# A backward scan in place of a reciprocal, and the early token sums moved into the low-rank products, in a hybrid HGRN2 and latent-attention layer

## The chip, the cores and the metric

The kernel runs on one core of a Trainium2 chip. The metric is the device time of one execution in microseconds (us). The engines are called PE (matrix products; PEld is its weight load), DVE (vector), ACT (scalar, with the function tables), POOL (GpSimd) and SP (which here only issues DMAs). A granted clock of 1.00 is PE at full speed.

## The reference

One decoder layer on 512 tokens of width 1024, all in 32-bit floats. The input is normalized and multiplied by one wide matrix, whose columns feed two branches and a merge:

```
h = rms_norm(x);  P = h @ w_in
f = lb + (1 - lb) * sigmoid(hf);  k = 1 - f;  q = silu(hq);  v = hi      # HGRN2, 8 heads of 128
b = cumsum(log f) inside each chunk of 32 tokens
q_in = q * exp(b);  k_in = k * exp(-b);  k_out = k * exp(b_last - b)
o = causal(q_in @ k_in^T) @ v + q_in @ state                            # state: over the chunks
y_a = rms_norm(o) * silu(z_a)
y_b = attention(c_q, c_kv, k_rope) * silu(z_b)                          # 8 heads, low-rank q and kv
m = sigmoid(g_a) * (y_a @ w_proj_a) + sigmoid(g_b) * (y_b @ w_proj_b)
out = x + m @ w_out
```

Along a token chunk, exp(b) is the running product of f, and exp(b_last - b) is the product of the f that come after a token up to the chunk's end.

## The kernel before, in words

Every product is made in three terms. A 32-bit matrix is split into a high part (a cast on ACT, L129 and L171) and a low part (what is left, on DVE, L130 and L172), and `mm3` issues high by high, high by low and low by high (L102 to L104). Normalized tokens lie transposed in `hT[0]` and `hT[1]`, the high and the low part, features on the partitions. Weights come by `load_w`: SP issues a load of 512 KB into one of three raw buffers (L123), ACT casts, DVE subtracts. Behind each load SP pops one DMA of a list `queued` (L790): a copy of a part of the merge's weights into DRAM scratch (`g_t`), to which POOL adds another part later, one `step()` at a time (L797). These sums of weights, and sums of token blocks, serve the merge products at the end, which are made by a scheme of the Strassen kind.

The order of the work: the norm with the first low-rank columns (c_q and a part of c_kv), written out by hand; then the "wide low-rank products", 448 columns more in four token tiles (`mm_ps` to `c_sb`, L400 is ACT's copy of a tile); the squares and norms of these (L405 on ACT, `power` on POOL, L418 on DVE); their transposes on PE (L422), cast and split into `cT` (L423 and L424); the rotated key part `kd` (L411 to L415 on POOL), its transposes (L428) and its split into `kpe`. Then come the HGRN heads, in four pairs, and after them the attention heads and the merge. Apart from the hand-ordered stretches, the scheduler of the kernel's framework sets the order on each engine, from the priorities of the program's order and a model of costs.

A pair of heads (`hg_pair`) makes the product of its forget columns F (two PSUM tiles of `mm_ps`, of which there are three in all), then `hg_forget` for both heads, then the values I (for four heads at a time), the query columns Q, `hg_query`, the state products, the gate columns ZA, the scores and the outputs. `hg_forget` goes so: tanh on ACT (L460) out of PSUM, `f` on DVE (L461), `k` on POOL (L463), the running product `pr` by a scan on DVE (L465), whose second operand `fr` restarts it at each chunk, its reciprocal over all 512 columns (L466), ten small POOL operations on the chunk ends (`gh`, `ft`), then `ki = k / pr` (L483), `ko = ki * last` (L484), `k64` and `k128`. The tile of tanh and the reciprocal share one buffer (`tf`), `f` and the query share another, so that the second head's tanh waits for the first head's `ki`. The scores use `ki` against `qi` within blocks of 64 tokens (L532), `ko` against `qi` from chunk to chunk, and `k64` against `q64`.

The tiles of the heads lie in a pool `hgrn`, among them `fr`, two `gh` and two `asb` (the score tiles, cleared once by POOL, L439 to L445). The pool's space is free early in the kernel, so these clearings run at 16 to 17.5 us.

`early_sums(q)` makes, for one half of the feature tiles, the sums of the token blocks of `hT` that the merge needs: four sums of high and low part (L820), four combinations (L773 and L777), a split of each into high and low, and eight stores of 256 KB from SP (L827). Its tiles are those of the attention's pool `mla_a`. The call for the first half stands in the first pair, where the other pairs call `step()`; that for the second half stands behind the first pair.

Of the kernel before, what the change touches and what calls it, by code (L numbers as in the profile page):

```python
# [24 lines left out]
C = 32  # L25
# [5 lines left out]
TINY = 1.1754944e-38  # L31
# [7 lines left out]
def hybrid_layer(ctx: ExitStack, tc: tile.TileContext, a):  # L39
    nc = tc.nc  # L40
# [11 lines left out]
    dram = ctx.enter_context(tc.tile_pool(name="dram", bufs=1, space=bass.MemoryType.DRAM))  # L52
# [114 lines left out]
    last_pool, last_dve, last_act = [None], [None], [None]  # L167

    def split(hi, lo, src):

        nc.scalar.copy(hi, src)  # L171
        nc.vector.tensor_tensor(lo, src, hi.bitcast(F32), op=ALU.subtract)  # L172
# [283 lines left out]
    def hg_forget(h, pf, meanwhile=None):  # L456

        gh = gh_[h % 2]
        tf, f, k = W("tf", 1), W("f", 1), W("k", 1)
        nc.scalar.activation(tf[:], pf[:], AF.Tanh, scale=0.5)  # L460
        nc.vector.tensor_scalar(f[:], tf[:], c1[:, h : h + 1], c2[:, h : h + 1], op0=ALU.mult, op1=ALU.add)  # L461
        nc.gpsimd.tensor_scalar(fr[:, ::C], f[:, ::C], TINY, None, op0=ALU.max)
        nc.gpsimd.tensor_scalar(k[:], tf[:], c1n[:, h : h + 1], c1[:, h : h + 1], op0=ALU.mult, op1=ALU.add)  # L463
        pr, rp = W("pr"), W("tf", 1)
        nc.vector.tensor_tensor_scan(pr[:], f[:], fr[:], 0.0, op0=ALU.mult, op1=ALU.max)  # L465
        nc.vector.reciprocal(rp[:], pr[:])  # L466
# [12 lines left out]
        last_pool[0] = g.tensor_tensor(ft[:], gh[:, :, 6], gh[:, :, 1], op=ALU.mult)
        if meanwhile:  # L480
            meanwhile()
        ki, ko, k128, k64 = W("ki"), W("ko"), W("k128"), W("k64", 2, (P, S // 2))
        nc.vector.tensor_tensor(ki[:], k[:], rp[:], op=ALU.mult)  # L483
        nc.vector.tensor_tensor(c3(ko), c3(ki), last.rearrange("p (n o) -> p n o", o=1).broadcast_to([P, S // C, C]), op=ALU.mult)  # L484
        last_pool[0] = g.tensor_tensor(c2_(k64), c4(ko)[:, :, 0:2], bc(gh, 8, 2), op=ALU.mult)
        nc.vector.tensor_tensor(c4(k128), c4(ko), bc(gh, 0, 4), op=ALU.mult)
        return pr, ft, ki, ko, k64, k128

    def hg_query(h, pq, pr, meanwhile=None):

        gh = gh_[h % 2]
        q = W("f", 1)
        last_act[0] = nc.scalar.activation(q[:], pq[:], AF.Tanh, scale=0.5)
        if meanwhile:
            meanwhile()
        nc.vector.scalar_tensor_tensor(q[:], q[:], 1.0, pq[:], op0=ALU.add, op1=ALU.mult)
# [4 lines left out]
        return qi, q64, q128  # L501

    n3 = (NT - 1) * P

# [20 lines left out]
    def hg_scores(heads):  # L525

        res = [(asb_[h % 2], ax_tile()) + t for h, t in heads]
        for _, aps, ki, ko, k64, qi, q64 in res:
# [5 lines left out]
        for _, aps, ki, ko, k64, qi, q64 in res:  # L534
# [5 lines left out]
        for asb, aps, ki, ko, k64, qi, q64 in res:  # L540
# [231 lines left out]
    def minus(out, x, y):
        nc.vector.tensor_tensor(out, x, y, op=ALU.subtract)  # L773

    def minus_minus(out, x, y):

        nc.vector.scalar_tensor_tensor(out, x, -1.0, y, op0=ALU.mult, op1=ALU.subtract)  # L777
# [33 lines left out]
    h_dram = [[dram.tile([P, 4, 256], F32, name=f"h{n}{i}") for i in range(2)] for n in range(1, 5)]  # L811

    def early_sums(q):

        E = lambda tag: ma_pool.tile([P, 2, 256], F32, tag)[:]
        h11, h12, h21, h22 = zip(*[[b[:, q] for b in blocks(t)] for t in hT])

        def whole(tag, hl):
            out = E(tag)
            nc.vector.tensor_tensor(out, hl[0].bitcast(F32), hl[1].bitcast(F32), op=ALU.add)  # L820
            return out

        def keep(n, tag, src):
            hl = Pair(ma_pool.tile([P, 2, 2, 256], F32R, tag)[:])
            split(*hl, src)
            for i in range(2):
                nc.sync.dma_start(h_dram[n - 1][i][:, q], hl[i].bitcast(F32))  # L827

        e22, e21, e11, e12 = whole("qr", h22), whole("qs", h21), whole("qh", h11), whole("p3", h12)
        minus(e22, e22, e21)  # L830
        keep(1, "qn", e22)
        minus_minus(e22, e22, e11)
        keep(2, "kn", e22)
        minus(e21, e11, e21)
        keep(3, "qp", e21)
        minus_minus(e12, e12, e22)
        keep(4, "qn", e12)
# [470 lines left out]
```

## Time and profile before

| | |
|---|---|
| median of 3 executions | 606.26 us (606.16 to 606.81) |
| the profiled execution | 606.53 us, of which the span is 604.7 us |
| mean granted clock of PE | 0.996 |
| PE busy | 595.2 us (98%) |
| DVE busy | 445.2 us (74%) |
| ACT busy | 283.0 us (47%) |
| POOL busy | 148.3 us (25%) |

The profile is a page with busy shares, and a trace that answers queries: waits (an engine's idle time by what ended it), stretches (busy time of each engine between two times), groups of instructions by line, and timelines. In a timeline row the first number is the start and the second the length in us, and in brackets stands the idle time of the engine before it, with what ended it. A matmul of 512 columns reads 0.39 us long, but the next one starts 0.23 us after it, since they overlap. Every time below is from the start of the span.

### The profile page before, as it was taken

How to read it: one execution, taken by the hardware profiler on the slowest of the kernel's cores; microseconds unless marked ns; L12 is line 12 of the kernel's file. 1: busy time of each engine (PE TensorE's matmuls, PEld its weight loads, DVE VectorE, ACT ScalarE, POOL GpSimd, SP SyncE). 2: the span in 40 equal slices, each digit the busy share in tenths (PEclk: the TensorE clock that was granted, in tenths of full speed). 3: DMA queues.
4: the chain of work that ended last, by engine and by line, in shares of the span. 5: the costliest groups of instructions: out<-in, count | busy, mean ns of one | idle time of the engine just before them, and what ended most of it. 6: DMA issues, size and time to landing. Idle time of an engine off the chain costs nothing.

```text
span 604.7 us, 8828 instructions
## 1 busy us (share of the span) xinstructions
PE 595.2 (98%) x3198; PEld 501.5 (83%) x3198; DVE 445.2 (74%) x689; ACT 283.0 (47%) x517; POOL 148.3 (25%) x253
## 2 busy tenths in 40 slices
PE   9999999999999999999999999999999999999994
PEld 6998888888888888888888888888888888888883
DVE  7717989599764548959767776778878878466795
ACT  7555245333313342436545554456557764153553
POOL 3107322254350237415245540400000000000003
PEclk9999999999999999999999999999999999999998
DMA  8449479997969967582369676888666656366313
GB/s 281 159 137 345 155 220 370 318 223 169 239 152 253 232 194 155 112 186 76 62 153 175 147 159 154 222 289 244 192 187 204 204 182 188 123 233 257 102 36 139
DMA packets 73036, 115.34 MB, mean 191 GB/s; under 512 B 7561, under 2 KB 37663, under 8 KB 72993
## 3 DMA queue, kind: packets, MB, share of 16 engines
q1 hardware_dynamic: 63740, 90.99, 47.2%
q0 software_dynamic: 8336, 22.55, 20.2%
q10 hardware_dynamic: 916, 1.25, 0.6%
q8 instruction: 25, 0.41, 0.3%
q14 instruction: 19, 0.15, 0.1%
HBM read 106.38 MB, written 39.85 MB: 242 GB/s over the span
## 4 chain that ended last, share of the span: by engine, by line
PE 89%; DVE 4%; DMA 3%; ACT 2%; issue 1%; POOL 1%; SPq 0%; POOLq 0%; ACTq 0%; DVEq 0%
PE mm_ps L102 19%; PE mm_ps L104 19%; PE mm_ps L103 19%; PE ax_ps L889 16%; PE mm_ps L889 3%; PE ax_ps L754 1%; PE ax_ps L728 1%; DMA x<-x 1%; PE mm_ps L282 1%; PE ax_ps L556 1%; DVE ya L1173 1%; PE ax_ps L558 1%; PE ax_ps L518 1%; PE ax_ps L104 1%; PE ax_ps L103 1%
## 5 line engine op out<-in xcount | busy, mean ns | idle before, releaser
L130 DVE TENSOR_TENSOR w_lo<-w_raw,w_hi 128x1024 fp32r<-128x1024 f32 (+3 forms) x116 | 138.9, 1204 | 68.9 <-ACT w_hi L129 66.1
L129 ACT CAST w_hi<-w_raw 128x1024 fp32r<-128x1024 f32 (+3 forms) x116 | 114.8, 1007 | 132.6 <-PE mm_ps L103 54.7
L102 PE MATMUL mm_ps<-hT,w_hi 128*128 128x512 f32 x256 | 101.0, 395 | 0.0
L103 PE MATMUL mm_ps<-hT,w_hi 128*128 128x512 f32 x256 | 100.3, 392 | 0.0
L104 PE MATMUL mm_ps<-hT,w_lo 128*128 128x512 f32 x256 | 100.2, 393 | 0.0
L102 PE MATMUL mm_ps<-w_hi,hT 128*128 128x512 f32 (+1 forms) x160 | 61.7, 390 | 0.0
L103 PE MATMUL mm_ps<-w_lo,hT 128*128 128x512 f32 (+1 forms) x160 | 61.5, 385 | 0.0
L104 PE MATMUL mm_ps<-w_hi,hT 128*128 128x512 f32 (+1 forms) x160 | 61.4, 385 | 0.0
L104 PEld LDWEIGHTS mm_ps<-hT,w_lo 128*128 128x128 f32 x256 | 48.1, 188 | 9.9
L102 PEld LDWEIGHTS mm_ps<-hT,w_hi 128*128 128x128 f32 x256 | 48.1, 188 | 9.5
L103 PEld LDWEIGHTS mm_ps<-hT,w_hi 128*128 128x128 f32 x256 | 48.1, 188 | 9.4
L889 PE MATMUL ax_ps<-w_hi,s 128*128 128x512 f32 x208 | 51.5, 389 | 0.0
L889 PEld LDWEIGHTS ax_ps<-w_hi,s 128*128 128x128 f32 x208 | 39.0, 188 | 8.1
L1190 POOL TENSOR_SCALAR ssum<-ssum 128x1 f32<-128x1 f32 x3 | 0.7, 225 | 163.7 <-ACT z L1177 163.6
L104 PEld LDWEIGHTS mm_ps<-w_hi,hT 128*128 128x128 f32 x160 | 30.1, 188 | 5.5
L102 PEld LDWEIGHTS mm_ps<-w_hi,hT 128*128 128x128 f32 x160 | 30.0, 188 | 5.2
L103 PEld LDWEIGHTS mm_ps<-w_lo,hT 128*128 128x128 f32 x160 | 30.1, 188 | 5.1
L736 ACT ACTIVATE p<-ax_ps,sm 128x128 f32<-128x128 f32 (+3 forms) x32 | 16.8, 526 | 35.6 <-DVE sm L735 35.4
L738 POOL TENSOR_SCALAR p<-p,sm 128x128 f32<-128x128 f32 (+3 forms) x28 | 15.6, 563 | 65.0 <-DVE sm L737 54.3
L889 PE MATMUL ax_ps<-w_lo,s 128*128 128x512 f32 x104 | 27.8, 389 | 0.0
L466 DVE RECIPROCAL tf<-pr 128x512 f32<-128x512 f32 x8 | 26.8, 3348 | 0.1
L889 PEld LDWEIGHTS ax_ps<-w_lo,s 128*128 128x128 f32 x104 | 19.5, 188 | 4.0
(319 smaller groups left out, 1189.1 us busy)
## 6 DMA issues: line engine op xcount, KB each, us to landing
w_raw<-w_in SPq DMA_DIRECT2D x54, 512.0 KB, 7.0
g_t<-w_in SPq DMA_DIRECT2D x16, 512.0 KB, 8.9
w_raw<-g_t SPq DMA_DIRECT2D x16, 512.0 KB, 4.7
g_t<-w_in POOLq DMA_DIRECT2D x8, 512.0 KB, 10.5
pa_t<-w_proj_a SPq DMA_DIRECT2D x8, 512.0 KB, 8.4
g_t<-g_t POOLq DMA_DIRECT2D x8, 512.0 KB, 10.0
out_t<-w_out SPq DMA_DIRECT2D x8, 512.0 KB, 9.6
s<-h POOLq DMA_DIRECT2D x8, 512.0 KB, 11.7
```

The source lines that it names most:

```text
L102: nc.tensor.matmul(ps, lh[lsl], rh[rsl], start=start, stop=False)
L103: nc.tensor.matmul(ps, lh[lsl], rl[rsl], start=False, stop=False)
L104: nc.tensor.matmul(ps, ll[lsl], rh[rsl], start=False, stop=stop)
L129: last_hi[0] = nc.scalar.copy(hi[:, :o], raw[:, :o])
L130: last_lo[0] = nc.vector.tensor_tensor(lo[:, :o], raw[:, :o], hi[:, :o].bitcast(F32), op=ALU.subtract)
L282: nc.tensor.matmul(ps, hT[l][:, 4 * kh + k, t * P : t * P + P], c_hl[kh][r][:, k * 256 : k * 256 + 256], start=kh == 0 and kind == 0 and k ...
L466: nc.vector.reciprocal(rp[:], pr[:])
L518: nc.tensor.matmul(sps[:, sl], kt_[:, sl], v_sb[i][:, (h % 4) * P : (h % 4) * P + P], start=True, stop=True)
L556: nc.tensor.matmul(ops[:, sl], asb[:, sl], v_sb[i][:, (h % 4) * P : (h % 4) * P + P], start=True, stop=i == 0)
L736: last_act[0] = nc.scalar.activation(p[:, :n], sps[:, :n], AF.Exp, scale=SCALE, bias=sm[:, 1:2], accum_out=sm[:, 2:3])
L738: scaled_p = (nc.vector if final else nc.gpsimd).tensor_scalar(p[:, :n], p[:, :n], sm[:, 3:4], 0.5, op0=ALU.mult, op1=ALU.mult)
L889: nc.tensor.matmul(ps[:, o : o + n], ap[i][:, k, t * P : t * P + P], w[k // 2][j][:, k % 2, o : o + n], start=fresh and c == 0, stop=c == ...
```

## The change

It has two parts. In `hg_forget` the reciprocal of `pr` goes. A second scan runs from right to left over `f`, shifted by one, with a second operand `ends` (a tiny number, and 1.0 at each chunk's last token), and gives `rest`, the product of the later `f` in the chunk. `ko` is `k * rest`. Only the 16 chunk ends of `pr` are inverted (`inv`), and the query side gets `qd = qi * inv`; the scores within 64 tokens are `ko` against `qd` in place of `ki` against `qi`, as many matmuls of the same sizes. `f` becomes one tile of the pool with 64 columns of 1.0 behind it. `rest` takes the buffer of tanh, as the reciprocal did.

In the second part `early_sums` stands ahead of the wide low-rank products, for both halves, in a pool `early_sums` of its own, which is closed at once. And `step()` is called behind the forgets of the first pair too, so that all of POOL's weight sums go one step earlier.

```diff
+    ep = Pool("early_sums", "left")
+    def early_sums(q):
...
+        E = lambda tag: ep.tile([P, 2, 256], F32, tag)[:]
...
+    for q in kh:
+        early_sums(q)
+    ep.close()
     for t2, ps in enumerate(c_ps):
...
     nc.gpsimd.memset(fr[:], TINY)
+    ends = hw.tile([P, S], F32, "ends")
+    nc.gpsimd.memset(ends[:], TINY)
+    nc.gpsimd.memset(ends[:, C - 1 :: C], 1.0)
+    f_ = hw.tile([P, S + 64], F32, "f_")
+    nc.gpsimd.memset(f_[:, S:], 1.0)
...
-        pr, rp = W("pr"), W("tf", 1)
-        nc.vector.tensor_tensor_scan(pr[:], f[:], fr[:], 0.0, op0=ALU.mult, op1=ALU.max)
-        nc.vector.reciprocal(rp[:], pr[:])
+        pr, rest, inv = W("pr"), W("tf", 1), W("inv", 2, (P, S // C))
+        nc.vector.tensor_tensor_scan(rest[:, ::-1], f_[:, S:0:-1], ends[:, ::-1], 0.0, op0=ALU.mult, op1=ALU.max)
+        nc.vector.tensor_tensor_scan(pr[:], f, fr[:], 0.0, op0=ALU.mult, op1=ALU.max)
         last = pr[:, C - 1 :: C]
         F = last.rearrange("p (g c) -> p g c", c=4)
+        nc.vector.reciprocal(inv[:], last)
...
-        ki, ko, k128, k64 = W("ki"), W("ko"), W("k128"), W("k64", 2, (P, S // 2))
-        nc.vector.tensor_tensor(ki[:], k[:], rp[:], op=ALU.mult)
-        nc.vector.tensor_tensor(c3(ko), c3(ki), last.rearrange("p (n o) -> p n o", o=1).broadcast_to([P, S // C, C]), op=ALU.mult)
+        ko, k128, k64 = W("ko"), W("k128"), W("k64", 2, (P, S // 2))
+        nc.vector.tensor_tensor(ko[:], k[:], rest[:], op=ALU.mult)
...
-        qi, q128, q64 = W("qi"), W("q128"), W("q64", 2, (P, S // 2))
-        nc.vector.tensor_tensor(qi[:], q[:], pr[:], op=ALU.mult)
+        qi, qd, q128, q64 = W("qi"), pr, W("q128"), W("q64", 2, (P, S // 2))
+        nc.vector.tensor_tensor(qi[:], q, pr[:], op=ALU.mult)
+        nc.vector.tensor_tensor(c3(qd), c3(qi), inv[:].rearrange("p (n o) -> p n o", o=1).broadcast_to([P, S // C, C]), op=ALU.mult)
...
-                    nc.tensor.matmul(aps[n * 64 : n * 64 + 64, b], ki[:, b], qi[:, b], start=True, stop=True)
+                    nc.tensor.matmul(aps[n * 64 : n * 64 + 64, b], ko[:, b], qd[:, b], start=True, stop=True)
...
-        if pair:
-            step()
-        else:
-            early_sums(kh[0])
+        step()
...
-        if pair == 0:
-            early_sums(kh[1])
```

How the instructions move is seen in the order in which they stand on each engine, with the line, the operation, the tiles and the semaphores that each waits for (those named DMAHW count landings of SP's transfers). The lines of the changed kernel are its own: its L508 is the tanh (L460 before), L466 the cast to `cT` (L423), L171 is the cast of `kpe` in both, and L420 is a store of the early sums.

First ACT, from the norm of the low-rank columns to the second head's tanh. Before:

```order
L405 ACTIVATE csq,css<-c_sb 128x256
L129 CAST w_hi<-w_raw 128x1024 [waits DMAHW1_49,DVE_49]
L129 CAST w_hi<-w_raw 128x1024 [waits DMAHW3_49,DVE_49,PE_49]
L460 ACTIVATE tf<-mm_ps 128x512 [waits PE_49]
L423 ACTIVATE cT_91<-ax_ps,par 128x512 [waits PE_49] x5
L129 CAST w_hi<-w_raw 128x1024 [waits DMAHW5_49,DVE_49,PE_49]
L171 CAST kpe<-ax_ps 128x512 [waits PE_49]
L460 ACTIVATE tf<-mm_ps 128x512 [waits DVE_49,Pool_49]
```

And now:

```order
L171 CAST kn<-qr 128x512 [waits DMAHW6_49,DMAHW5_49,DVE_49]
L129 CAST w_hi<-w_raw 128x1024 [waits DMAHW6_49,PE_49]
L171 CAST qn<-p_473 128x512 [waits DMAHW7_49,DMAHW4_49,DVE_49]
L129 CAST w_hi<-w_raw 128x1024 [waits DMAHW1_49,PE_49]
L466 ACTIVATE cT_91<-ax_ps,par 128x512 [waits PE_49] x5
L171 CAST kpe<-ax_ps 128x512 [waits PE_49]
L508 ACTIVATE tf<-mm_ps 128x512 [waits DMAHW6_49,DMAHW3_49,DVE_49]
L646 COPY v_859<-mm_ps 128x512 [waits PE_49]
L508 ACTIVATE tf<-mm_ps 128x512 [waits DVE_49,Pool_49]
```

The first head's tanh stood ahead of the five casts to `cT` and of the cast of `kpe`, and stands behind them now; and it waits for stores (of the second `kn`), since its tile lies where that one lay.

PE has the same instructions as before, matmul for matmul. Of their order, one thing matters here: the places at which it waits for ACT's two tanh. Before, 12 matmuls of the value products (tiles `mm_ps`, one for 128 tokens) stood ahead of the transposes of `kd`, and 22 do now; two more matmuls follow, and then the value tile `mm_ps_864`. It takes the PSUM buffer of the first head's forget tile, so its first matmul waits for the first head's tanh. 33 matmuls later the first one of `mm_ps_944`, in the buffer of the second forget tile, waits for the second head's tanh.

On POOL the clearings stood ahead of all of `kd`. Before:

```order
L177 TENSOR_TENSOR rs<-rs,fixed 128x1 [waits Pool_49]
L439 MEMSET fr 128x512
L443 MEMSET gh_632 128x48
L445 MEMSET asb_634 128x512
L443 MEMSET gh_636 128x48
L445 MEMSET asb_638 128x512
L411 TENSOR_TENSOR kd<-c_sb,ktab 128x4x64 [waits DMAHW6_49,Activation_49]
```

Now they stand behind it and behind the load of `qtab`:

```order
L479 DMA qtab<-c_qtab 128x1024
L482 MEMSET fr 128x512 [waits DVE_49]
L484 MEMSET ends 128x512
L487 MEMSET f__711 128x64 [waits DVE_49]
L491 MEMSET gh_713 128x48
L493 MEMSET asb_715 128x512 [waits DMAHW5_49,DMAHW4_49,DMAHW7_49,DMAHW2_49,DMAHW0_49]
L491 MEMSET gh_717 128x48
L493 MEMSET asb_719 128x512
L511 TENSOR_SCALAR k<-tf,c1n,c_418 128x512 [waits DMAHW5_49,DMAHW6_49,DMAHW3_49,Activation_49]
L485 MEMSET ends 128x16 [waits Pool_49]
L510 TENSOR_SCALAR fr<-f__711 128x16 [waits DVE_49]
```

The first `asb` waits for five stores from the place where it lies now, the last ones of SP's row among them; the first head's `k`, and the strided clearing of `ends` that the backward scan waits for, stand behind it.

SP's row, from the second load of the first pair's values on, had loads and copies by turns. Now stores stand between them:

```order
L123 DMA w_raw<-w_in 128x2x512
L420 DMA h_424<-qn 128x512
L826 DMA g_t_722<-w_in 128x2x512
L123 DMA w_raw<-w_in 128x2x512
L420 DMA h_425<-qn 128x512
L826 DMA g_t_723<-w_in 128x2x512
L123 DMA w_raw<-w_in 128x2x512
L826 DMA g_t_723<-w_in 128x2x512
L420 DMA h_426<-kn 128x512
L123 DMA w_raw<-w_in 128x4x256
L826 DMA g_t_724<-w_in 128x2x512
L420 DMA h_427<-kn 128x512
```

Behind these rows stand one more store, a load and a copy, and then the last store, for which the first `asb` waits.

More of the change, by code (lines that the diff above doesn't have):

```diff
@@ L390, in hybrid_layer, with minus, minus_minus, whole @@
     nc.vector.tensor_scalar(c2[:], lb[:], 0.5, 0.5, op0=ALU.mult, op1=ALU.add)
+    kh = [slice(0, 2), slice(2, 4)]
+    half_t = [slice(0, 256), slice(256, 512)]
+    blocks = lambda t: (t[:, 0:4, half_t[0]], t[:, 4:8, half_t[0]], t[:, 0:4, half_t[1]], t[:, 4:8, half_t[1]])
+    def minus(out, x, y):
+        nc.vector.tensor_tensor(out, x, y, op=ALU.subtract)
+    def minus_minus(out, x, y):
+        nc.vector.scalar_tensor_tensor(out, x, -1.0, y, op0=ALU.mult, op1=ALU.subtract)
+    h_dram = [[dram.tile([P, 4, 256], F32, name=f"h{n}{i}") for i in range(2)] for n in range(1, 5)]
+    ep = Pool("early_sums", "left")
+    def early_sums(q):
+        E = lambda tag: ep.tile([P, 2, 256], F32, tag)[:]
+        h11, h12, h21, h22 = zip(*[[b[:, q] for b in blocks(t)] for t in hT])
+        def whole(tag, hl):
+            out = E(tag)
+            nc.vector.tensor_tensor(out, hl[0].bitcast(F32), hl[1].bitcast(F32), op=ALU.add)
+            return out
+        def keep(n, tag, src):
+            hl = Pair(ep.tile([P, 2, 2, 256], F32R, tag)[:])
+            split(*hl, src)
+            for i in range(2):
+                nc.sync.dma_start(h_dram[n - 1][i][:, q], hl[i].bitcast(F32))
+        e22, e21, e11, e12 = whole("qr", h22), whole("qs", h21), whole("qh", h11), whole("p3", h12)
+        minus(e22, e22, e21)
+        keep(1, "qn", e22)
+        minus_minus(e22, e22, e11)
+        keep(2, "kn", e22)
+        minus(e21, e11, e21)
+        keep(3, "qp", e21)
+        minus_minus(e12, e12, e22)
+        keep(4, "qn", e12)
+    for q in kh:
+        early_sums(q)
+    ep.close()
     for t2, ps in enumerate(c_ps):
@@ L458, in hg_forget @@
         gh = gh_[h % 2]
-        tf, f, k = W("tf", 1), W("f", 1), W("k", 1)
+        tf, k, f = W("tf", 1), W("k", 1), f_[:, :S]
         nc.scalar.activation(tf[:], pf[:], AF.Tanh, scale=0.5)
-        nc.vector.tensor_scalar(f[:], tf[:], c1[:, h : h + 1], c2[:, h : h + 1], op0=ALU.mult, op1=ALU.add)
+        nc.vector.tensor_scalar(f, tf[:], c1[:, h : h + 1], c2[:, h : h + 1], op0=ALU.mult, op1=ALU.add)
         nc.gpsimd.tensor_scalar(fr[:, ::C], f[:, ::C], TINY, None, op0=ALU.max)
         nc.gpsimd.tensor_scalar(k[:], tf[:], c1n[:, h : h + 1], c1[:, h : h + 1], op0=ALU.mult, op1=ALU.add)
-        pr, rp = W("pr"), W("tf", 1)
-        nc.vector.tensor_tensor_scan(pr[:], f[:], fr[:], 0.0, op0=ALU.mult, op1=ALU.max)
-        nc.vector.reciprocal(rp[:], pr[:])
+        pr, rest, inv = W("pr"), W("tf", 1), W("inv", 2, (P, S // C))
+        nc.vector.tensor_tensor_scan(rest[:, ::-1], f_[:, S:0:-1], ends[:, ::-1], 0.0, op0=ALU.mult, op1=ALU.max)
+        nc.vector.tensor_tensor_scan(pr[:], f, fr[:], 0.0, op0=ALU.mult, op1=ALU.max)
         last = pr[:, C - 1 :: C]
         F = last.rearrange("p (g c) -> p g c", c=4)
+        nc.vector.reciprocal(inv[:], last)
         g = nc.gpsimd
@@ L481, in hg_forget, with hg_query @@
             meanwhile()
-        ki, ko, k128, k64 = W("ki"), W("ko"), W("k128"), W("k64", 2, (P, S // 2))
-        nc.vector.tensor_tensor(ki[:], k[:], rp[:], op=ALU.mult)
-        nc.vector.tensor_tensor(c3(ko), c3(ki), last.rearrange("p (n o) -> p n o", o=1).broadcast_to([P, S // C, C]), op=ALU.mult)
+        ko, k128, k64 = W("ko"), W("k128"), W("k64", 2, (P, S // 2))
+        nc.vector.tensor_tensor(ko[:], k[:], rest[:], op=ALU.mult)
         last_pool[0] = g.tensor_tensor(c2_(k64), c4(ko)[:, :, 0:2], bc(gh, 8, 2), op=ALU.mult)
         nc.vector.tensor_tensor(c4(k128), c4(ko), bc(gh, 0, 4), op=ALU.mult)
-        return pr, ft, ki, ko, k64, k128
-    def hg_query(h, pq, pr, meanwhile=None):
+        return pr, ft, inv, ko, k64, k128
+    def hg_query(h, pq, pr, inv, meanwhile=None):
         gh = gh_[h % 2]
-        q = W("f", 1)
-        last_act[0] = nc.scalar.activation(q[:], pq[:], AF.Tanh, scale=0.5)
+        q = f_[:, :S]
+        last_act[0] = nc.scalar.activation(q, pq[:], AF.Tanh, scale=0.5)
         if meanwhile:
             meanwhile()
-        nc.vector.scalar_tensor_tensor(q[:], q[:], 1.0, pq[:], op0=ALU.add, op1=ALU.mult)
-        qi, q128, q64 = W("qi"), W("q128"), W("q64", 2, (P, S // 2))
-        nc.vector.tensor_tensor(qi[:], q[:], pr[:], op=ALU.mult)
+        nc.vector.scalar_tensor_tensor(q, q, 1.0, pq[:], op0=ALU.add, op1=ALU.mult)
+        qi, qd, q128, q64 = W("qi"), pr, W("q128"), W("q64", 2, (P, S // 2))
+        nc.vector.tensor_tensor(qi[:], q, pr[:], op=ALU.mult)
+        nc.vector.tensor_tensor(c3(qd), c3(qi), inv[:].rearrange("p (n o) -> p n o", o=1).broadcast_to([P, S // C, C]), op=ALU.mult)
         last_pool[0] = nc.gpsimd.tensor_tensor(c2_(q64), c4(qi)[:, :, 2:4], bc(gh, 10, 2), op=ALU.mult)
         last_dve[0] = nc.vector.tensor_tensor(c4(q128), c4(qi), bc(gh, 4, 4), op=ALU.mult)
-        return qi, q64, q128
+        return qd, qi, q64, q128
     n3 = (NT - 1) * P
@@ L527, in hg_scores @@
         res = [(asb_[h % 2], ax_tile()) + t for h, t in heads]
-        for _, aps, ki, ko, k64, qi, q64 in res:
+        for _, aps, ko, k64, qd, qi, q64 in res:
             for i in range(NT):
@@ L531, in hg_scores @@
                     b = slice(i * P + n * 64, i * P + n * 64 + 64)
-                    nc.tensor.matmul(aps[n * 64 : n * 64 + 64, b], ki[:, b], qi[:, b], start=True, stop=True)
-        for _, aps, ki, ko, k64, qi, q64 in res:
+                    nc.tensor.matmul(aps[n * 64 : n * 64 + 64, b], ko[:, b], qd[:, b], start=True, stop=True)
+        for _, aps, ko, k64, qd, qi, q64 in res:
             for i in range(NT):
@@ L539, in hg_scores @@
                                      start=True, stop=True)
-        for asb, aps, ki, ko, k64, qi, q64 in res:
+        for asb, aps, ko, k64, qd, qi, q64 in res:
             for i in range(NT):
@@ L603, in hg_pair @@
         pq = proj_ch(w_in, COL_Q + cc, hT)
-        qq = [hg_query(h, pq[i], kk[i][0], None if i else in_query) for i, h in enumerate(hs)]
+        qq = [hg_query(h, pq[i], kk[i][0], kk[i][2], None if i else in_query) for i, h in enumerate(hs)]
         step()
@@ L612, in scores @@
         def scores():
-            return hg_scores([(h, kk[i][2:5] + qq[i][0:2]) for i, h in enumerate(hs)])
+            return hg_scores([(h, kk[i][3:5] + qq[i][0:3]) for i, h in enumerate(hs)])
         def outs(aa):
-            on = [hg_out(h, aa[i], sts[i], qq[i][2], v_sb) for i, h in enumerate(hs)]
+            on = [hg_out(h, aa[i], sts[i], qq[i][3], v_sb) for i, h in enumerate(hs)]
             step()
@@ L764, in mla_out @@
         nc.vector.tensor_tensor(yb[:, h], ops[:], z[:], op=ALU.mult)
-    kh = [slice(0, 2), slice(2, 4)]
-    half_t = [slice(0, 256), slice(256, 512)]
-    blocks = lambda t: (t[:, 0:4, half_t[0]], t[:, 4:8, half_t[0]], t[:, 0:4, half_t[1]], t[:, 4:8, half_t[1]])
     TERMS = ((0, 0), (1, 1), (0, 1), (1, 0))
[L772 to L777, printed above, removed]
     class BlockSums:
@@ L810, in hybrid_layer @@
     out_w = BlockSums("out", a["w_out"][0])
[L811 to L837, printed above, removed]
     adds = [(gate_w[0], 0), (gate_w[0], 2), (gate_w[1], 0), (gate_w[0], 1), (gate_w[1], 2), (gate_w[0], 3), (gate_w[1], 1),
```

## The prediction

> **What bounds the kernel now.** I read the page first, for the busy shares, then the waits of PE, then the stretches around the two edits, and last the timeline of each engine from 40 to 75 us. The page:
>
> ```profile
> span 604.7 us, 8828 instructions
> PE 595.2 (98%) x3198; PEld 501.5 (83%) x3198; DVE 445.2 (74%) x689; ACT 283.0 (47%) x517; POOL 148.3 (25%) x253
> ```
>
> All waits of PE in the trace, with us in total, times and the longest:
>
> ```profile
> PE ax_ps L247 <- DVE zero L293: 1.2, 1, 1.2
> PE ax_ps L271 <- DVE xn L263: 0.2, 1, 0.2
> PE ax_ps L889 <- DVE ya L1173: 0.2, 1, 0.2
> ```
>
> Stretches (busy PE, PEld, DVE, ACT and POOL, then PE's clock, the DMA share and GB/s):
>
> ```profile
> 30.00:60.00 30.00, 30.00 (x152) 26.57 (x151) 13.36 (x20) 15.92 (x32) 10.67 (x21) 1.00 0.73 240
> 45.00:60.00 15.00, 15.00 (x78) 12.72 (x77) 10.52 (x15) 8.03 (x14) 10.67 (x21) 1.00 1.02 341
> 60.00:75.00 15.00, 15.00 (x70) 12.40 (x69) 15.00 (x20) 3.63 (x7) 5.91 (x12) 1.00 0.45 153
> ```
>
> PE is full in every stretch, also from 60 to 75 us, where DVE has no idle time at all: DVE is crowded, but PE doesn't wait for it. Outside the three waits, 1.6 us together, PE is idle only at the very start and after its last matmul. PE's instructions are the same in number and size after the change. So the change has next to nothing to win: the 1.2 us wait for `zero` lies ahead of all edits, and 0.4 us is left. It can lose, wherever it makes PE wait.
>
> **First edit: the scan for the reciprocal.**
>
> ```profile
> L466 DVE RECIPROCAL tf<-pr 128x512 f32<-128x512 f32 x8 | 26.8, 3348 | 0.1
> L465 DVE TENSOR_TENSOR_SCAN pr<-f,fr 128x512 f32<-128x512 f32 x8 | 9.8, 1223 | 6.5 <-POOL fr L462 6.5
> L483 DVE TENSOR_TENSOR ki<-k,tf 128x512 f32<-128x512 f32 x8 | 5.5, 682 | 0.0
> L484 DVE TENSOR_TENSOR ko<-ki,pr 128x512 f32<-128x512 f32 x8 | 5.5, 687 | 0.1
> ```
>
> Eight reciprocals go (26.8 us); eight scans like the present one come (9.8). `ki` goes (5.5), `qd` comes, a product with a broadcast factor like `ko` (5.5). The reciprocal of 16 columns has no row; a 32nd of 3.35 us is 0.1, and a tenth of the long one, 0.3, is its other end, so 1 to 2.7 us for eight. DVE gains 14 to 16 us in eight places. None ends a wait of PE, so the path gains 0, at most the 0.4 us above. The scores read `ko` and `qd` in place of `ki` and `qi`; they stand far behind them, so this costs nothing. The end mask costs POOL a memset of 0.53 us and two small ones, once.
>
> **Second edit: the early sums.** The first half's sums and splits go from 65 us and later to the wide products, into idle time of DVE (13.36 busy of 30) and ACT (15.92). That is free in itself. But SP now carries 16 stores there, and the sums have a pool of their own, whose space the heads' tiles take over afterwards. Two places come of it where PE now stands behind a chain.
>
> *First wait, kpe and tanh.* These are the transposes of `kd`, the next matmuls, and ACT's cast:
>
> ```profile
> 60.36 0.60 PE L428 MATMUL ax_ps<-ident,kd 128*128 128x128 f32 x4
> ...
> 61.27 0.40 PE L104 MATMUL mm_ps<-w_hi,hT 128*128 128x512 f32 x1
> ...
> 61.00 0.59 ACT L171 CAST kpe<-ax_ps 128x512 fp32r<-128x512 f32 x1 [2.35 <-PE ax_ps L428]
> 65.31 0.60 ACT L460 ACTIVATE tf<-mm_ps 128x512 f32<-128x512 f32 x1 [3.72 <-DVE ki L483]
> ```
>
> By the new order the transposes stand ten matmuls later, at about 60.36 + 10 x 0.23 = 62.6 = s. Two matmuls follow, and PE is at `mm_ps_864` at s + 0.91 (60.36 to 61.27, with the transposes and two matmuls between). That matmul waits for the first tanh, which now stands on ACT behind the cast of kpe: cast from s + 0.64 (61.00 less 60.36), 0.59 long, tanh 0.60, so s + 1.83. PE waits 0.9 us at 63.5.
>
> *Second wait, the stores.* Once the last early store has landed, at a time L, POOL can clear the first `asb`; behind that stand the second `gh`, the second `asb`, `k` and the strided clearing of `ends`. DVE's backward scan waits for this last one, then comes the forward scan, then `ko`; the second head's tanh waits for `ko` (same buffer), and `mm_ps_944` for the tanh. The rows, each the operation itself or its nearest:
>
> ```profile
> 16.46 0.53 POOL L445 MEMSET asb<- 128x512 f32 x1
> ...
> 17.00 0.53 POOL L445 MEMSET asb<- 128x512 f32 x1
> ...
> 53.60 1.81 POOL L463 TENSOR_SCALAR k<-tf,c1n,c 128x512 f32<-128x512 f32 x1 [1.53 <-ACT tf L460]
> 55.48 0.29 POOL L462 TENSOR_SCALAR fr<-f 128x16 f32<-128x16 f32 x1
> ...
> 157.86 1.03 POOL L463 TENSOR_SCALAR k<-tf,c1n,c 128x512 f32<-128x512 f32 x1 [7.03 <-ACT tf L460]
> ```
>
> Clearing: 16.46 to 17.53 = 1.07. `k` is 1.03 or 1.81; I take 1.03, because DVE waits at that time and POOL is alone. Strided clearing 0.29, two scans 2.45, `ko` 0.69, tanh 0.60. Sum 6.1: PE goes on at L + 6.1.
>
> Now L. The first of these loads, ACT's cast that waited for it, and POOL's load of `qtab`:
>
> ```profile
> 43.66 0.37 SPq L123 DMA_DIRECT2D w_raw<-w_in  x1
> ...
> 47.48 1.05 ACT L129 CAST w_hi<-w_raw 128x1024 fp32r<-128x1024 f32 x1 [1.18 <-DMA w_raw<-w_in]
> 58.39 0.79 POOL L436 DMA_DIRECT2D qtab<-c_qtab  x1
> ```
>
> The load issued at 43.66 had landed at 47.48 (ACT waited for it). At 341 GB/s, the rate of the stretch 45 to 60, where the DMA share is 1.02, 512 KB take 1.54 us, so its bytes began to flow at 45.9. From this load to the last early store SP's new order holds five loads and five copies of 512 KB and six stores of 256 KB; the 512 KB of `qtab` are issued on POOL about when `kd` is done, so among them. That is 14 times 512 KB or 7.34 MB, and 21.5 us at 341 GB/s. The flow starts later than before, since a cast and a DVE operation of the early sums stand ahead of the weights' split that frees the buffer:
>
> ```profile
> 70.34 0.62 ACT L171 CAST qn<-qr 128x512 fp32r<-128x512 f32 x1 [1.22 <-DVE qr L773]
> 65.13 0.68 DVE L820 TENSOR_TENSOR qr<-hT,hT 128x512 f32<-128x512 f32 x1
> 71.05 0.39 PE L102 MATMUL mm_ps<-w_hi,hT 128*128 128x512 f32 x1
> ```
>
> 0.62 + 0.68 = 1.3 us, so L = 45.9 + 1.3 + 21.5 = 68.7. Ends: 65.7 (start only 0.6 later, `qtab` later than the stores, and 356 GB/s, the best of the row below) and 71 (start 2.6 later, since that cast waits for stores too, and 329).
>
> ```profile
> 45.00:50.00 5.00, 5.00 (x24) 4.14 (x23) 2.13 (x2) 2.32 (x6) 4.42 (x7) 1.00 0.98 329
> 55.00:60.00 5.00, 5.00 (x29) 4.29 (x28) 4.19 (x3) 3.62 (x6) 2.78 (x12) 1.00 1.04 356
> ```
>
> The Trainium skill, DMA: Bandwidth & Descriptors, section "Issuing engines are not separate DMA queues", says that transfers started by different engines run on the same 16 DMA engines and interleave. By it the copy of `qtab` counts in L (68.7); with a queue of its own beside SP's, L would be 67.2. No row of this trace separates the two.
>
> The matmul `mm_ps_944` has as many matmuls and transposes ahead of it as the one that started at 71.05. PE goes on there at 68.7 + 6.1 = 74.8, so the two waits together cost 3.8 us, 0.9 in the first and 2.9 in the second. Behind them nothing gives it back, because PE is full to the end. The loss lies between 0.9 (L under 65.9) and 71 + 6.9 - 71.05 = 6.9 us (with `k` at 1.81).
>
> **The weight sums** on POOL go one step earlier. They are issued behind `k64` of the second head, so `k128`, and behind it DVE's split of the next weights, wait for POOL's issues. These are the second half of the query's weights, which PE reaches 63 matmuls of 0.23 us behind `mm_ps_944`, 14 us. From the tanh to `ko` it is `k` 1.03, clearing 0.29, two scans 2.45 and 0.69, 4.5 us, so two issues of 0.79 (as `qtab`) have 8 us of cover. I cost this at 0; without the cover it is 1.6 us.
>
> **Sum.** The profiled execution took 606.53 us, 0.3 above the median of 606.26. 606.53 + 3.8 = 610.3 for it, and 606.26 + 3.8 = 610.1 from the median, which is my forecast.
>
> **Rivals.** (a) The stores land in time. If L is under 65.9, the second wait is gone, and only the 0.9 us of kpe and tanh are left: 607.2. That is not slower by what can be told here. A measurement of this kernel separates about 0.2%, or 1.2 us. For it: the DMA share of 0.73 from 30 to 60 us, so the transfers have room ahead of 45, and stores that are issued there are over early. Against it: the last six stand behind loads, and from 45 on the share is 1.02.
>
> (b) PE's clock falls. The second wait of 2.9 us is about as long as the idle time after which the clock fell at the end of this trace:
>
> ```profile
> 596.00:597.00 1.00, 0.98 (x9) 0.77 (x7) 0.97 (x3) 0.66 (x3) 0.28 (x1) 1.00 1.02 422
> ...
> 599.00:600.00 1.00, 0.00 (x0) 0.00 (x0) 0.46 (x1) 0.46 (x1) 0.51 (x1) 0.99 0.71 277
> 600.00:601.00 1.00, 0.00 (x0) 0.00 (x0) 0.09 (x1) 0.15 (x1) 0.00 (x0) 0.50 0.69 266
> ```
>
> PE ended at 597.0 and the clock was 0.50 from 600.0. If it comes back after as long a time, 3 us of matmuls at half speed lose 1.5: 611.6. The Trainium skill, TensorE: Matmul & The Clock Gate, section "Part 1: The HAM clock gate (the "warmup" mystery)", has this rule: an idle window of about 3.4 us sets the clock to half and a busy one lifts it, and the windows run freely. By it a wait under 3.4 us doesn't lower the clock, and one that does loses an estimated 1.7 us. The 3.0 us of this trace are a little under its window.
>
> (c) The freed DVE time shows after all: the change doesn't slow anything, PE's 0.4 us vanish, 605.9, or a little less if short gaps of PE close that the waits don't list. For it: DVE at 15.00 of 15 from 60 to 75. Against it: PE at 15.00 there.
>
> (d) The DMA queue is later still, L over 71: above 612.8.
>
> **How the numbers follow.** Two waits as worked out, 608 to 611.6: 0.62. (b) 0.15. (d) 0.03. (a) 0.13, within 0.2%. (c) 0.07, of which 0.04 faster by over 0.2% and 0.03 within. So slower 0.80, same 0.16, faster 0.04. The range runs from (a), 607.2, to 606.26 + 6.5 = 612.8, just short of the late end of 6.9; outside lie (c) and (d).
>
> **What would show it.** In the profile after: a wait of PE for ACT's `tf` at about 63.5 us, 0.9 long, and a second one, about 2.9, at 72; POOL's first `asb` clearing from 60 to 70 us, ended by a DMA `h<-qn`; the clock at 1.00 behind it; DVE some 15 us less busy, with PE's busy time unchanged. I am wrong if PE has no new wait, or if `asb` is cleared before 66 us; if PE loses time behind 80 us, I missed a place.

## The result, and the profile after

The changed kernel took 611.68 us (median of 6 executions, 610.46 to 613.07), the kernel before 606.72 on the same chips (606.16 to 608.04). The ratio is 1.0084, 95% interval 1.0073 to 1.0095: 5.1 us slower. Ratios here are taken over the executions of both kernels and are not exactly the quotient of the two medians. The forecast was 610.1, in a range of 607.2 to 612.8.

The page of the changed kernel; its profiled execution took 613.07 us:

```profile
span 611.3 us, 8848 instructions
...
PE 597.6 (98%) x3198; PEld 502.1 (82%) x3198; DVE 433.7 (71%) x697; ACT 282.0 (46%) x517; POOL 158.1 (26%) x256
```

DVE is 11.5 us less busy than before, and PE 2.4 us busier with as many instructions. PE's waits:

```profile
PE mm_ps L102 <- ACT tf L508: 4.1, 2, 2.1
PE ax_ps L247 <- DVE zero L293: 1.2, 1, 1.2
PE ax_ps L271 <- DVE xn L263: 0.4, 2, 0.2
PE ax_ps L896 <- DVE ya L1180: 0.4, 1, 0.4
PE ax_ps L465 <- DVE c_sb L461: 0.2, 1, 0.2
```

The first row is new: two waits for tanh, of 2.0 and 2.1 us. The chain to each, from the timelines of PE, ACT and POOL (L471 are the transposes of `kd`):

```profile
62.99 0.60 PE L471 MATMUL ax_ps<-ident,kd 128*128 128x128 f32 x4
66.06 0.50 PE L102 MATMUL mm_ps<-w_hi,hT 128*128 128x512 f32 x1 [2.00 <-ACT tf L508]
75.90 0.79 PE L102 MATMUL mm_ps<-w_hi,hT 128*128 128x512 f32 x1 [2.05 <-ACT tf L508]
76.49 0.63 PE L103 MATMUL mm_ps<-w_lo,hT 128*128 128x512 f32 x1
...
79.40 0.40 PE L104 MATMUL mm_ps<-w_hi,hT 128*128 128x512 f32 x1
```

```profile
63.62 0.59 ACT L171 CAST kpe<-ax_ps 128x512 fp32r<-128x512 f32 x1 [2.29 <-PE ax_ps L471]
65.41 0.60 ACT L508 ACTIVATE tf<-mm_ps 128x512 f32<-128x512 f32 x1 [1.19 <-DMA h<-kn]
...
75.25 0.60 ACT L508 ACTIVATE tf<-mm_ps 128x512 f32<-128x512 f32 x1 [8.76 <-DVE ko L532]
```

```profile
70.06 0.53 POOL L493 MEMSET asb<- 128x512 f32 x1 [10.75 <-DMA h<-qn]
```

The first tanh stands behind the cast of `kpe`, which ended at 64.2, and then waited 1.19 us more for a store of `kn`. The second tanh stands behind the chain from `asb`, which POOL could clear only when the last store of `qn` had landed, at 70.0. The middle of this chain:

```profile
71.85 0.12 POOL L485 MEMSET ends<- 128x16 f32 x1
72.00 1.23 DVE L513 TENSOR_TENSOR_SCAN tf<-f__711,ends 128x512 f32<-128x512 f32 x1 [5.42 <-POOL ends L485]
74.49 0.67 DVE L532 TENSOR_TENSOR ko<-k,tf 128x512 f32<-128x512 f32 x1
```

From the clearing of `asb` to PE's next matmul it is 5.84 us.

After the second wait the matmuls start 0.43 us apart (76.49 to 76.92 and on), not 0.23. The stretches, of 3.4 us each, show why (the columns are those of the prediction's stretches):

```profile
62.30:65.70 3.40, 1.75 (x10) 1.14 (x8) 1.84 (x3) 0.88 (x2) 0.00 (x0) 1.00 1.07 392
65.70:69.10 3.40, 3.04 (x13) 2.53 (x14) 0.55 (x1) 0.78 (x2) 0.00 (x0) 1.00 1.05 389
69.10:72.50 3.40, 3.40 (x16) 2.82 (x16) 0.50 (x1) 0.00 (x0) 2.36 (x6) 1.00 0.32 121
72.50:75.90 3.40, 1.35 (x7) 0.77 (x6) 2.72 (x5) 0.65 (x2) 2.08 (x8) 1.00 0.00 0
75.90:79.30 3.40, 3.40 (x8) 2.72 (x9) 2.45 (x3) 0.86 (x2) 3.32 (x7) 0.50 0.01 2
79.30:82.70 3.40, 3.40 (x16) 2.77 (x16) 3.30 (x5) 1.67 (x2) 2.08 (x3) 1.00 0.00 0
```

From 75.9 to 79.3 the granted clock is 0.50. Eight matmuls take 3.50 us there (75.90 to 79.40), where 8 times 0.227 = 1.82 would do: 1.7 us. With the waits, 4.1 + 1.7 = 5.8 us; 0.2 more at the transposes of `c_sb`, and 0.4 in longer waits at the start and the end. That is 6.4 of the 6.5 us between the two profiled executions (613.07 and 606.53). The medians are only 5.0 apart, since this profiled execution is the longest of its six; how the loss of the others divides into waits and clock is not recorded.

### The profile page after: what moved, and what is told of

It is laid out like the page before. It is cut to its first block, busy times and chain, and to the rows that moved or that the text cites. A ratio compares the mean times of both kernels' runs of the same rounds, so it can differ in the third digit from the quotient of the medians.

```text
span 611.3 us, 8848 instructions
## 1 busy us (share of the span) xinstructions
PE 597.6 (98%) x3198; PEld 502.1 (82%) x3198; DVE 433.7 (71%) x697; ACT 282.0 (46%) x517; POOL 158.1 (26%) x256
## 4 chain that ended last, share of the span: by engine, by line
PE 86%; DVE 5%; DMA 4%; ACT 2%; issue 1%; POOL 1%; SPq 0%; POOLq 0%; ACTq 0%; DVEq 0%
PE mm_ps L102 18%; PE mm_ps L103 18%; PE mm_ps L104 18%; PE ax_ps L896 16%; PE mm_ps L896 3%; DMA h<-qn 2%; PE ax_ps L800 1%; PE ax_ps L774 1%; DMA x<-x 1%; PE mm_ps L282 1%; PE ax_ps L605 1%; DVE ya L1180 1%; PE ax_ps L607 1%; PE ax_ps L567 1%; PE ax_ps L104 1%
## 5 line engine op out<-in xcount | busy, mean ns | idle before, releaser
L102 PE MATMUL mm_ps<-w_hi,hT 128*128 128x512 f32 (+1 forms) x160 | 63.0, 396 | 4.1 <-ACT tf L508 4.1
L104 PE MATMUL mm_ps<-w_hi,hT 128*128 128x512 f32 (+1 forms) x160 | 62.1, 388 | 0.0
L548 POOL TENSOR_TENSOR q<-qi,gh 128x256 f32<-128x256 f32 x8 | 6.9, 867 | 53.1 <-DVE qi L546 53.1
```

Source lines behind the costliest of these rows:

```text
L102: nc.tensor.matmul(ps, lh[lsl], rh[rsl], start=start, stop=False)
L104: nc.tensor.matmul(ps, ll[lsl], rh[rsl], start=False, stop=stop)
```

## The experiments

**1. The scan alone.** The early sums and `step()` are put back:

```diff
-    for q in kh:
-        early_sums(q)
-    ep.close()
...
-        step()
+        if pair:
+            step()
+        else:
+            early_sums(kh[0])
...
+        if pair == 0:
+            early_sums(kh[1])
```

> The backward scan alone: the early sums and step() stay where they were before. Theory (stores and the order behind them make PE wait): none of the new waits is there, DVE is some 15 us less busy, PE's waits stay at about 1.6 us, the time is that of before, 606.7 within 1 us. Rival (the scan itself, by ko waiting for both scans and k, delays the second head's tanh): a wait of PE for tanh of 1 us or more is there too, 608 or above.

606.83 against 606.71 us, ratio 0.9996 (0.9987 to 1.0005). No new wait, and in the page of this kernel DVE is 15 us less busy than in that of before:

```profile
PE 595.0 (98%) x3198; PEld 501.2 (83%) x3198; DVE 430.1 (71%) x697; ACT 282.7 (47%) x517; POOL 159.7 (26%) x256
```

So the first edit gives DVE 15 us and the kernel nothing. The rival that the scan itself delays tanh falls.

**2. The early sums alone.** The reciprocal is kept; the sums stand ahead of the wide products, and `step()` is called in the first pair:

```diff
+    ep = Pool("early_sums", "left")
...
+    for q in kh:
+        early_sums(q)
+    ep.close()
...
-        if pair:
-            step()
-        else:
-            early_sums(kh[0])
+        step()
...
-        if pair == 0:
-            early_sums(kh[1])
```

> The early sums moved and step() added, the reciprocal kept. The heads' tiles lie otherwise here, and the first head's tanh lies where the last stores read. Theory: the last store lands at 69 to 70 us, tanh ends 0.6 later, PE is ready at 64, so it waits 6 to 7 us in one place, and its clock falls once behind it (1.7 us): 606.7 + 8.5 = 615. Rival (the sums cost by crowding DVE and ACT, not by the place of their tiles): about as much as with both edits, 611.7 or less.

616.02 us, ratio 1.0142 (1.0123 to 1.0161), 8.6 us slower: the theory's size, and not the rival's. PE's longest wait in its trace, and ACT's row for this tanh:

```profile
PE mm_ps L102 <- ACT tf L503: 5.4, 1, 5.4
```

```profile
69.81 0.60 ACT L503 ACTIVATE tf<-mm_ps 128x512 f32<-128x512 f32 x1 [4.63 <-DMA h<-qn]
```

It is 5.4 us, not 6 to 7, and some small waits come to it (0.8, 0.7 and 0.7 us). By the fewer tiles of this kernel, tanh itself lies over the last stores, of `qn`; in the changed kernel the first tanh lies over those of `kn`, and only `asb` over the last ones. Which tile lies there decides how much is lost; the layout that came with the scan's tiles made it less.

**3. The tiles laid out otherwise.** Both edits, and the late tiles of `hgrn` are put where the stores read:

```diff
     hw = Pool("hgrn", "right")
+    for tag, n, w in (("qi", 2, S), ("q128", 2, S), ("q64", 2, S // 2), ("kt", 2, 384), ("st", 2, 384), ("k64", 2, S // 2)):
+        hw.tile([P, w], F32, tag, n)
```

> Both edits; the tiles of the pool hgrn that are used late (qi, q128, q64, kt, st, k64) are laid out first, so that they and not tanh, k and asb lie where the early stores read. The order on PE and ACT is that of the changed kernel. Theory: the wait for the stores goes, asb is cleared at 56 us, the second wait of 2.0 us and the fallen clock go, and of the first wait of 2.0 us the 0.9 stay that kpe ahead of tanh costs: 606.7 + 0.9 + 0.3 = 607.9. Rival (POOL's and DVE's chain is long by itself): a second wait of 1 us or more stays, 609.5 or above.

609.11 us, ratio 1.0034 (1.0020 to 1.0047), 2.1 us slower than before and, by the two ratios, 3 us faster than the change (2.6 by the medians). Its waits, and its first clearing of `asb`:

```profile
PE ax_ps L465 <- DVE c_sb L461: 1.1, 2, 0.8
PE mm_ps L102 <- ACT tf L510: 0.7, 1, 0.7
```

```profile
56.71 0.51 POOL L495 MEMSET asb<- 128x512 f32 x1
```

With the same order of instructions on PE and ACT, the second wait is gone and with it the rival that POOL's and DVE's chain is too long by itself, and 0.7 of the first is left, near the 0.9 for `kpe` ahead of tanh. The median is 1.2 over the expectation, by a wait of 1.1 at the transposes of `c_sb`, which I had not counted. POOL's chain to the norm of `c_sb` begins later now, 46.29 against 45.33, since ACT's copy stands behind casts of the early sums, and its first step is longer, 1.81 against 1.17 us (1.80 in this run). Why it is longer is open. The row of the changed kernel, and of the kernel before:

```profile
46.29 1.81 POOL L454 TENSOR_TENSOR kd<-c_sb,ktab 128x256 f32<-128x256 f32 x1 [30.72 <-ACT c_sb L443]
```

```profile
45.33 1.17 POOL L411 TENSOR_TENSOR kd<-c_sb,ktab 128x256 f32<-128x256 f32 x1 [27.80 <-ACT c_sb L400]
```

**4. The same layout, `step()` as before.** Run later, beside experiment 10.

```diff
-        step()
+        if pair:
+            step()
         def gate():
```

> The tiles laid out so that the stores are in nobody's way, and step() not called behind the first pair's forgets. Theory: the waits of the kernel with that layout (0.7 for kpe ahead of tanh, 1.1 at the transposes of c_sb) have nothing to do with the weight sums and stay: 608.9 within 1 us. Rival: the weight sums had a part in its 2.1 us: 607.5 or less.

608.72 us, ratio 1.0040 (1.0027 to 1.0052). The same two waits, 1.1 and 0.7. The weight sums have no part in them.

**5. Idle matmuls in the second wait.** Nine matmuls into a spare tile, right ahead of the one that waits; their result is not used:

```diff
...
+                    if k == 2:
+                        spare = ax_tile()
+                        for n in range(fill):
+                            with tc.issue_after(mm_last[0].ins):
+                                mm_last[0] = nc.tensor.matmul(spare[:], hT[0][:, n % KD, 0:P], hT[0][:, n % KD], start=n == 0, stop=n == fill - 1)
+                        with tc.issue_after(mm_last[0].ins):
+                            part(1, 0)
...
```

> Both edits, and nine matmuls of 512 columns into a spare PSUM tile, ahead of the matmul that waits the second time (work that is of no use; 9 times 0.227 = 2.04 us, the length of the wait). If the fallen clock behind the wait comes from PE's idle time: clock 1.00 through 74 to 80 us, matmuls of 0.23 us there, and 1.7 us less than the changed kernel, 610.0. Rival (the slow matmuls have another cause, or the clock falls by the sum of both waits): the clock falls all the same, 611.7 or above.

One of its six executions read 1508 us, for which no cause was found; the median of the other five is 612.24 us, ratio 1.0097 (1.0078 to 1.0116). The matmuls ran from 72.63 to 74.7, and PE went on at 74.78, right behind the tanh; without them it would have idled about 1.9 us. The clock stayed at 1.00, as the stretch shows:

```profile
75.00:80.00 5.00, 5.00 (x23) 4.10 (x23) 3.94 (x5) 2.32 (x3) 3.60 (x7) 1.00 0.01 2
```

But no time was won. A new wait stands in the list of this kernel, and the two rows of POOL and DVE ahead of it show where it comes from:

```profile
PE mm_ps L106 <- DVE w_lo L132: 1.9, 1, 1.9
```

```profile
81.70 2.42 POOL L849 DMA_DIRECT2D g_t<-w_in  x2
...
84.39 0.69 DVE L550 TENSOR_TENSOR k<-ko,gh 128x512 f32<-128x512 f32 x1 [3.80 <-POOL gh L537]
```

POOL issues two weight sums, 2.42 us, ahead of the small products that `k128` waits for. In this kernel the split of the query's first weights stands on DVE behind `k128`; in the changed kernel it stands ahead of it. So the run fits the theory that the idle time lowers the clock, but doesn't show what the clock costs. Nor does it settle the first by itself: the first wait of the changed kernel, of 2.0 us, did not lower the clock either.

**6 and 7. `step()` as before, without and with the idle matmuls.** The edit of both is that of experiment 4, on the changed kernel and on experiment 5.

> Both edits, but step() is not called behind the forgets of the first pair, so POOL issues no weight sum there. Theory: PE has its two waits of 2.0 us and the fallen clock as before; k128 of the second head comes some 2.4 us earlier, and nobody waits for it, so the time is that of the changed kernel, 611.7 within 1 us. Rival (the earlier weight sums are part of the loss): 610.5 or less.

> The nine idle matmuls ahead of the second wait, and step() as it was before. In the run with the matmuls alone, the clock stayed at 1.00, but PE lost 1.9 us later, at the query's low weights, whose split stood on DVE behind k128, and that behind two DMA issues on POOL (2.4 us). Theory: without those issues this wait goes too, and the kernel is 1.7 us (the clock's part) under the changed kernel, 610.0. Rival (PE would lose the clock's 1.7 us anyway, at some other wait behind it): 611.5 or above.

Without the matmuls 612.0 us, ratio 1.0073 (1.0048 to 1.0098); with them 610.16, ratio 1.0046 (1.0029 to 1.0063). The weight sums by themselves make no difference here that the run can tell; the two waits in this trace are 0.9 and 2.7 us. With the weight sums out of the way, the idle matmuls win 1.8 us by the medians, near the 1.7 of the slow matmuls. The two intervals overlap, and in the profiled execution the matmuls ended at 76.48, 0.7 us after the tanh that PE waited for, so the times don't settle what the clock costs. That it fell without them and not with them, the clocks show; the mean granted clock of the six executions is 0.995 to 0.997 without them and 0.996 to 0.998 with them. First the kernel without them, after the wait of 2.7 us, then the one with them, both in the stretch of 75 to 80 us:

```profile
75.00:80.00 5.00, 4.20 (x12) 3.39 (x13) 3.38 (x6) 2.13 (x3) 4.53 (x12) 0.66 0.01 2
```

```profile
75.00:80.00 5.00, 5.00 (x24) 4.14 (x23) 3.38 (x5) 2.13 (x3) 4.48 (x12) 1.00 0.01 2
```

**8. Each store of the second half twice.**

```diff
             for i in range(2):
-                nc.sync.dma_start(h_dram[n - 1][i][:, q], hl[i].bitcast(F32))
+                for _ in range(1 if q.start == 0 else 2):
+                    nc.sync.dma_start(h_dram[n - 1][i][:, q], hl[i].bitcast(F32))
```

> Both edits, and each store of the second half issued twice to the same place: eight transfers of 256 KB more, of which six stand between the loads, 0.77 us each. Theory (the second wait is set by the landing of the last store): asb is cleared 4.6 to 6 us later, at 75 to 76, PE goes on at 81 to 82, and the time is 5 us above the changed kernel, 616.5 to 618. Rival (the queue has room, or POOL's chain alone sets it): less than 2 us more, under 613.7.

619.96 us, ratio 1.0210 (1.0192 to 1.0228), 8 us over the changed kernel and above the 616.5 to 618 expected:

```profile
PE mm_ps L102 <- ACT tf L509: 9.6, 2, 8.4
```

```profile
77.70 0.53 POOL L494 MEMSET asb<- 128x512 f32 x1 [12.26 <-DMA h<-qn]
```

`asb` is cleared 7.6 us later, and PE goes on at 83.55, again 5.85 us behind it. All eight extra stores may count (8 times 0.77 = 6.2 us); SP also waits 6.4 us for an older transfer among its last four stores. I had the place of the loss wrong: the first wait took 8.4 us of it, because the stores of `kn` are late as well, and the second only 1.2. The clock took more than before, too:

```profile
67.84:71.25 3.41, 0.00 (x0) 0.00 (x0) 0.00 (x0) 0.00 (x0) 0.00 (x0) 0.50 1.08 332
71.25:74.66 3.41, 2.32 (x6) 1.85 (x7) 0.55 (x1) 1.07 (x2) 0.00 (x0) 0.50 0.73 281
74.66:78.07 3.41, 3.41 (x10) 2.65 (x9) 0.00 (x0) 0.00 (x0) 0.37 (x1) 0.50 0.40 156
78.07:81.48 3.41, 3.41 (x16) 2.81 (x15) 1.71 (x2) 0.00 (x0) 2.81 (x6) 1.00 0.00 0
```

PE worked at half clock from 72.34 to 78.07, which loses 2.9 us, not 1.7. Between the two profiled executions, 620.05 and 613.07, that is 5.5 us more in the two waits and 1.2 more by the clock.

**9 and 10. Half of the early sums moved, with and without the earlier `step()`.** Only the first half stands ahead of the wide products; the second half stands where it was. Experiment 10 has the edit of experiment 4 besides.

```diff
-    def early_sums(q):
+    def early_sums(q, ep):
...
-    for q in kh:
-        early_sums(q)
+    early_sums(kh[0], ep)
     ep.close()
...
+        if pair == 0:
+            early_sums(kh[1], ma_pool)
```

> Both edits, but only the first half of the early sums stands ahead of the wide products; the second half stands behind the first pair in the attention's pool, where it was before. The last store from under the heads' tiles then lands before 45 us, and by the order the first tanh stands ahead of cT and kpe again. Theory: no new wait of PE, 606.7 within 1 us. Rival (early sums crowd ACT, DVE or the DMA queue around 40 to 50 us by themselves): a wait at the forget columns or the transposes of c_sb, 607.7 or above.

> As with half of the early sums moved, and step() not called behind the first pair's forgets. There, PE lost 1.0 us at 95 us because a load of the query's weights, issued at 79.8, landed only at 90, beside two weight sums that POOL had issued at 74.7. Theory (the earlier weight sums crowd the DMA queue there): without them no wait is left, 606.9 within 1 us. Rival (the second half's stores crowd it by themselves): the wait stays, 608 or above.

With the earlier `step()` 608.52 us, ratio 1.0036 (1.0020 to 1.0052); without it 606.64, ratio 1.0004 (0.9995 to 1.0013). The first has none of the waits for tanh, but it missed the 606.7 that was expected: its trace has a wait at a place that neither the theory nor the rival named, for the query, behind a load that was issued at 79.76 and that ACT waited for until 90:

```profile
PE mm_ps L102 <- DVE f__679 L543: 1.0, 1, 1.0
```

```profile
90.08 1.05 ACT L129 CAST w_hi<-w_raw 128x1024 fp32r<-128x1024 f32 x1 [8.99 <-DMA w_raw<-w_in]
```

Without the weight sums issued at 74.65 this wait is gone. The same load, issued at 79.61, had landed by 83.58:

```profile
83.58 1.05 ACT L129 CAST w_hi<-w_raw 128x1024 fp32r<-128x1024 f32 x1 [2.38 <-DMA w_raw<-w_in]
```

Of the twelve executions of the first, four took 610.3 to 611.5 us, one 609.5, the others 607.5 to 608.7; the profiled one is the shortest of them, so what the longer ones lose is open.

No kernel here is faster than the one before. Experiments 1 and 10, with the scan and, in 10, half of the sums moved, take as long as it.

## Why the prediction was right, point by point

*What bounds the kernel.* PE, with nothing to win elsewhere: right. Fifteen us less on DVE changed nothing (experiment 1). In the changed kernel it is 11.5 us less, since the moved sums add some: with them alone DVE is busy 447.9 us against 445.2 (experiment 2).

*First edit at 0.* Right. The scan, the small reciprocals (248 ns each, within the 0.1 to 0.3 us taken) and `qd` have cover.

*First wait, 0.9 us.* The part for `kpe` ahead of tanh is 0.7 (experiment 3). The wait was 2.0, because the tanh also waits for stores of `kn`: it is in the order shown ahead of the prediction, but I put a landing time only on the last store. The mistake doesn't show in the time: where PE goes on behind the second wait is set by the last store, so what the first wait gained, the second lost.

*Second wait, 2.9 us; L = 68.7.* The last store landed at 70.0, and the chain behind it took 5.84 us against 6.1. PE went on at 75.9, forecast 74.8. The two waits together are 4.1, forecast 3.8; more of them than I thought lies in the first. The other 0.8 of these 1.1 us is not in the two waits: 0.4 lies in waits ahead of them (0.2 more at the start, 0.2 at the transposes of `c_sb`); and a wait is counted from the end of the last matmul, 0.39 us behind its start, where the next one would have started after 0.23, so each costs nearly 0.2 more than it reads. Experiments 3 and 8 show that the store's landing sets the second one. L is 1.3 later than the sum, and 2.8 later than the 67.2 without `qtab`. The Trainium skill, DMA: Bandwidth & Descriptors, section "Issuing engines are not separate DMA queues", by which `qtab` shares the engines, is nearer to it, but other terms of L were off by as much, so the trace agrees without proving it. The term that was short is the number of bytes. From 45.9 to 70.06 the rate was the 341 GB/s that I took, which is 8.2 MB and not 7.3: SP's next load and copy, another 1.05 MB, were issued behind the last store and, by this sum, moved in the same time.

```profile
60.16 0.44 SPq L420 DMA_DIRECT2D h<-qn  x1
60.89 0.38 SPq L123 DMA_DIRECT2D w_raw<-w_in  x1
62.74 1.08 SPq L826 DMA_DIRECT2D g_t<-w_in  x1
```

*The weight sums at 0.* In the changed kernel this holds (experiment 6). The cover of 8 us is weaker than I wrote. Two issues took 2.42 us and not 1.6, and where the split of the query's weights stands behind `k128`, they cost a wait of 1.9 us (experiment 5). With half of the sums moved they cost about 1.9 by the ratios, 1.0 of it a wait in the trace for a load that landed late (experiments 9 and 10).

*The clock.* Here the working failed: the sum holds no term for it. Rival (b) had the mechanism, but I gave it 0.15, since 3.0 us passed at the end of the trace before the clock fell. It fell after an idle time of 2.05 us, and stayed down for 3.4 us. That is 1.7 us, where rival (b) took 1.5. The profiled execution lost 6.5 us where 3.8 were forecast, and the clock is the largest part of these 2.7. By the ratio, the loss was 5.1 us, between the forecast's 3.8 and rival (b)'s 5.3; and 0.5 of the 1.6 us between 610.1 and 611.7 is only that the kernel before took 606.72 beside this result, and not 606.26. That the measured time lay inside the range owes something to luck: the range reached to 612.8 for a late landing, and not for the clock.

*Left out:* the wait at the transposes of `c_sb`, 0.2 us in the changed kernel and up to 1.1 in others. Of the signs named in the prediction, the new waits and the clearing of `asb` behind `h<-qn` came; the clock at 1.00 behind it and PE's unchanged busy time did not.

## What to carry to other kernels

Work moved into idle time brings its stores along, and a buffer pool that is closed early hands their landing times on to whatever is laid over it: look at which tile lies there and what stands behind its first write. On a saturated engine a chain that comes late once costs all that it is late by, and nothing later gives it back; laying the late tiles out first took two lines and won 3 us. A short wait of PE can cost nearly as much again in the clock behind it (2.05 and 1.7 us here).

## What the runs showed of the hardware

The clock fell after less idle time than expected. In the changed kernel's stretches of 3.4 us above, one with 1.75 us of PE work was followed by a clock of 1.00, one with 1.35 us by 0.50, and after one full stretch it was 1.00 again. In stretches of 0.05 us the clock falls between 75.85 and 75.90 and rises between 79.25 and 79.30, 3.4 us later. The early sums alone show the same times: PE was idle from 65.0, and in its trace the clock is 0.50 from 70.1 to 73.5. The 3.4 us ahead of the stretches below hold 1.7 us of work (63.3 to 65.0), and it did not fall behind them.

```profile
66.70:70.10 3.40, 0.00 (x0) 0.00 (x0) 0.00 (x0) 0.29 (x1) 0.00 (x0) 1.00 1.00 371
70.10:73.50 3.40, 3.05 (x7) 2.47 (x8) 2.06 (x3) 0.78 (x2) 1.58 (x5) 0.50 0.14 55
```

The Trainium skill, TensorE: Matmul & The Clock Gate, section "Part 1: The HAM clock gate (the "warmup" mystery)", has free-running windows of about 3.4 us, and an idle window as the condition. The spacing agrees with these traces; the condition does not, since a window with 1.35 us of work, 40%, was enough to lower the clock. So a wait under 3.4 us is not safe, and whether one of 2 us costs the clock depends, as these traces read, on how it lies in the window: the first wait, as long as the second, lay across two of them and cost nothing. Where the limit lies between 1.35 and 1.7 us of work, no run shows.

A low clock is not always over after 3.4 us. In the run with the doubled stores, it stayed at 0.50 behind a stretch with 2.32 us of work, and rose only behind a full one, 10.2 us after it fell.
